# Two of the four weight sums of every pair, made by accumulating transfers of GpSimd instead of by VectorE

## The chip, the cores and the metric

The kernel runs on one core of a Trainium2 chip. The metric is the device time of one execution in microseconds (us). The time before is the median of three runs, 1945.45 us (1944.91 to 1946.29).

The core has five engines with instruction streams of their own: PE (the matrix engine), DVE (VectorE), ACT (ScalarE), POOL (GpSimd) and SP (SyncE, which here only issues transfers). Each takes its instructions in order and waits at semaphores for the others. Transfers are issued by an engine and carried out by 16 DMA engines.

## The reference

Two layers of a decoder trunk for 512 tokens and 1024 channels, all in fp32. Each layer projects the normed input once, runs three token mixers beside each other, merges them by gates, and ends in a feed-forward part of four times the width:

```
h = rms_norm(x, norm1[l]) * (1.0 + sc1) + sh1
proj = h @ w_in[l]
q, k, v, g, u, vs, p, gate_cols = split_columns(proj)
y_ret  = retention(q, k, v, g, positions)
y_sgu  = spatial_gating(u, vs, ws_gmlp[l], bs_gmlp[l], vnorm_gmlp[l])
y_pool = multiscale_pool(p, w_pool[l], b_pool[l], pool_scale[l])
branch_proj = einsum('bsnc,ncd->bsnd', stack([y_ret, y_sgu, y_pool]), w_branch[l])
gates  = sigmoid(gate_cols.reshape(B, S, 3, D_MODEL))
x = x + gt1 * (sum(gates * branch_proj) @ w_out[l])
h2 = rms_norm(x, norm2[l]) * (1.0 + sc2) + sh2
x = x + gt2 * (square(relu(h2 @ w_ff1[l])) @ w_ff2[l])
```

The modulation vectors sc1, sh1, gt1 and so on are products of a conditioning vector with w_ada.

## The kernel before

**Weights as units.** All weights stream from HBM in units of 128 partitions x 1024 values (512 KB), in the order in which they are used, on SP's queue (`load_raw`, L229, its transfer in L237). Each fp32 product is made of three faster ones (`mm3`, L401, its matmul in L407), so every unit and every activation is split in two: ACT copies the high half (`whi`), then DVE subtracts it from the raw values to get the low half (`wlo`; `split_unit`, L243). A plain unit gives one 128-column block of the output; it takes 24 matmuls of 512 columns.

**Pairs.** Two neighbouring units of the gates and of most of the first feed-forward matrix are computed together with seven half-size products in place of eight, by a scheme of sums (44 pairs, 22 per layer). With r1 and r2 as the two raw units and a, b as their left and right halves, DVE makes four sums of 128 x 512 (L218 in the profile, since all go through the helper `ttn`): s[a] = r2[a] + r2[b]; s[b] = s[a] - r1[a]; then in place r1[a] = r1[a] - r2[a] and r1[b] = r1[b] - s[b]. Four things are split per pair, in four groups: r1 as loaded (W1a, W1b), s (S1, S2), the changed r1 (S3, S4), and r2[b] (W2b). The activations have sums of the same kind, T1 to T4 (`Halved.add`, L139; the tiles `tpart`). `pair` (L419) runs the products in the order W1a, S1, S2, W1b, S3, S4, W2b, twelve matmuls of 256 columns each, into PSUM tiles a and d (`ps`) and b and c (`us`); between them ACT copies a into b (`us<-ps`) and b into c, and DVE adds d to b and to c (`gate<-us,d` or `pair<-us,d`).

**What sets the order.** The steps of a layer are listed (`step`), and `run` (L323) emits them one by one, with a look-ahead of two units or groups: `load_until` issues loads and splits ahead of the products, and the modulation units (`mod`, one DVE product over a whole unit in L257, then two or three small operations of `finish_mod`, on POOL for two columns of layer 0 at the start, else on DVE) are mixed in. From this the framework's scheduler fixes one instruction order per engine. Gates of the second branch come as single pairs between plain units. Those of the third begin with one pair and then three that stand together, and the pairs of the feed-forward matrix stand in runs of three, four and three. In such runs the last groups of one pair are split while the sums of the next are made.

**Pools.** Raw units rotate through 4 buffers (`wraw`), split units through 4, s through 1 (`sums`), small 512-column tiles through 8 (`tmp`). A load into a buffer waits until its last reader is done.

Of the kernel before, what the change touches and what calls it, by code (L numbers as in the profile page):

```python
# [11 lines left out]
F32 = mybir.dt.float32  # L12
F32R = mybir.dt.float32r
I32 = mybir.dt.int32
AF = mybir.ActivationFunctionType
ALU = mybir.AluOpType

P = 128
D = 1024
# [72 lines left out]
class Split:  # L92


    def __init__(self, pool, name):
        self.pool, self.name = pool, name
        self.t = {}
# [34 lines left out]
class Halved:  # L132
# [6 lines left out]
    def add(self, p, f=None):  # L139

        b = self.b
        if f is None:
            f = []
            for k2 in (p, p + KB // 4):
                f.append(b.b4("f32"))
                hi, lo = (self.act.two(w, k2).bitcast(F32) for w in ("hi", "lo"))
                b.ttn(f[-1], hi, lo, ALU.add)
        upper, lower = f
        r11, r12, r21, r22 = upper[:, :, :HT], upper[:, :, HT:], lower[:, :, :HT], lower[:, :, HT:]
        raws = [b.b4("tsum").rearrange("p a (k s) -> p a k s", k=2) for _ in range(2)]  # L150
        t1, t2, t3, t4 = (raws[i // 2][:, i % 2] for i in range(4))
        b.ttn(t1, r12, r11, ALU.subtract)
        b.ttn(t2, r22, t1, ALU.subtract)
        b.ttn(t3, r22, r12, ALU.subtract)
        b.ttn(t4, r21, t2, ALU.subtract)
        for names, raw in zip((("T1", "T2"), ("T3", "T4")), raws):
            hi, lo = (b.big.tile([P, 2, 2, HT], F32R, tag="b4", name=b.name("tpart")) for _ in range(2))
            b.act(hi, raw, AF.Copy)
            b.ttn(lo, raw, hi.bitcast(F32), ALU.subtract)
            for i, n in enumerate(names):  # L160
                self.sums[n, p] = [t[:, i] for t in (hi, lo)]
# [9 lines left out]
class Builder:  # L171
    def __init__(self, tc, ctx, ins, out, wstream, order):
        self.tc, self.nc = tc, tc.nc
        self.ins, self.out = ins, out
        self.wstream = wstream
        self.order = order
        self.steps = []
        self.const = ctx.enter_context(tc.tile_pool(name="const", bufs=1))
        self.big = ctx.enter_context(tc.tile_pool(name="big", bufs=BIG_BUFS))
        self.wraw = ctx.enter_context(tc.tile_pool(name="wraw", bufs=4))  # L180
        self.whl = ctx.enter_context(tc.tile_pool(name="whl", bufs=UNIT_BUFS))
        self.sums = ctx.enter_context(tc.tile_pool(name="sums", bufs=1))
        self.dram = ctx.enter_context(tc.tile_pool(name="dram", bufs=1, space=bass.MemoryType.DRAM))
        self.tmp = ctx.enter_context(tc.tile_pool(name="tmp", bufs=8))
        self.psum = ctx.enter_context(tc.tile_pool(name="psum", bufs=6, space=bass.MemoryType.PSUM))
        self.seeded = ctx.enter_context(tc.tile_pool(name="seeded", bufs=2, space=bass.MemoryType.PSUM))
        self.n_t = 0
# [82 lines left out]

    def load_pair(self, keys):

        r1, r2 = (self.load_raw(k) for k in keys)
        a, b = slice(0, S), slice(S, D)
        got = []

        def make(group):
            if group == 0:
                return self.split_unit(r1)
            if group == 1:  # L280
                s = self.sums.tile([P, D], F32, tag="sum", name=self.name("sum"))
                got.append(s)
                self.ttn(s[:, a], r2[:, a], r2[:, b], ALU.add)
                self.ttn(s[:, b], s[:, a], r1[:, a], ALU.subtract)
                return self.split_unit(s)
            if group == 2:
                self.ttn(r1[:, a], r1[:, a], r2[:, a], ALU.subtract)
                self.ttn(r1[:, b], r1[:, b], got[0][:, b], ALU.subtract)
                return self.split_unit(r1)
            return self.split_unit(r2[:, b])  # L290

        return make

# [125 lines left out]
    def pair(self, form, mov, out, f, hooks={}):  # L419

        a, b, c, d = (x()[:, :HT] for x in (self.bank, self.ubank, self.ubank, self.bank))
        h0, h1 = HALVES
        d_sb = self.tt("d")[:, h0]

        def product(ps, w, m, start):  # L430
            if w in hooks:
                hooks[w]()
            hi, lo = form(w)
            for j in range(KB // 2):
                o = slice(j * P, (j + 1) * P)
                self.mm3(ps, hi[:, o], lo[:, o], *mov.parts(m, j), start and j == 0, j == KB // 2 - 1, loose=True)

        product(a, "W1a", "R11", True)
        self.act(b, a, AF.Copy)
        product(d, "S1", "T1", True)  # L440
        self.act(d_sb, d, AF.Copy)
        product(b, "S2", "T2", False)
        self.act(c, b, AF.Copy)
        product(a, "W1b", "R21", False)
        f(out[:, 0, h0], a)
        product(b, "S3", "T3", False)
        self.ttn(out[:, 1, h1], b, d_sb, ALU.add)
        product(c, "S4", "R22", False)
        self.ttn(out[:, 0, h1], c, d_sb, ALU.add)
        product(b, "W2b", "T4", False)  # L450
        f(out[:, 1, h0], b)
# [747 lines left out]
    def final(self, i, units, between=None):  # L1199
        nc = self.nc  # L1200
        tok = HALVES[i]

        def pair(k2):
            def f():
                t = self.b4("fo")[:, :, tok]
                for j in range(2):
                    kb = 2 * k2 + j
                    self.stt(t[:, j, :], self.x[kb][:, tok], self.vecs[:, V_FN + kb:V_FN + kb + 1], ALU.mult,
                             self.rstd[:, tok], ALU.mult)
                o = self.out[k2 * 2 * P:(k2 + 1) * 2 * P, tok].rearrange("(a p) s -> p a s", p=P)  # L1210
                nc.sync.dma_start(out=o, in_=t)
            return f

        pair(0)()
        if between is not None:
            between()
        return [pair(k2) for k2 in range(1, KB // 2)]
# [91 lines left out]
```

## Time and profile before

| what | value |
|---|---|
| median of 3 runs | 1945.45 us |
| the profiled execution | 1946.67 us, span 1945.0 us |
| DMA packets | 77803, 263.18 MB |
| HBM read, written | 246.81 MB, 14.68 MB |
| q1 (all that SP issues) | 261.52 MB, 41.5% of 16 engines |

The page of the profile gives busy times of each engine, 40 slices of the span, the queues, the chain that ended last and the costliest groups. In a row of a group, the numbers behind the bar are busy us and mean ns of one, and behind a second bar the idle time just before them with what ended most of it. In a row of the timeline, the numbers are start and duration in us, and a bracket at the end holds the idle time before it and its releaser. Rows of DMA issues end in the size of one and the median us from issue to landing. Names are tiles of the program without their numbers.

### The profile page before, as it was taken

What the parts mean: (1) busy time and instruction counts of PE and PEld (TensorE: products, weight loads), DVE (VectorE), ACT (ScalarE), POOL (GpSimd) and SP (SyncE); (2) the same over time, 40 slices, a digit from 0 to 9 for tenths busy, and PEclk for the clock granted to TensorE, in tenths of its full rate; (3) what the DMA queues carried; (4) which work ended last, traced back from release to release, by engine and by line L of the source; (5) the groups of instructions that cost most, each with busy time, mean ns of one, the idle gap of its engine ahead of it and who ended that gap; (6) DMA issues with size and microseconds to landing.
All of it is one profiled execution on the core that took longest, in us unless ns stands there. A gap on an engine that the chain in (4) does not pass through costs nothing.

```text
span 1945.0 us, 25939 instructions
## 1 busy us (share of the span) xinstructions
PE 1923.6 (99%) x10424; PEld 1656.4 (85%) x10424; DVE 1291.9 (66%) x1913; ACT 814.7 (42%) x1156; POOL 19.9 (1%) x46
## 2 busy tenths in 40 slices
PE   8999999999999999999999999999999999999998
PEld 5889977888888888898888898778889898899896
DVE  7888657776864776676555775676587557455555
ACT  4444323443443544363434333334335337254452
POOL 2000000000000000000000000000000000000000
PEclk9999999999999999999999999999999999999999
DMA  9454633373242353453425456313523424232331
GB/s 354 152 173 152 214 112 108 108 251 118 98 152 87 106 176 108 152 164 119 130 87 180 145 182 202 114 55 108 185 84 111 141 79 149 87 120 72 124 98 54
DMA packets 77803, 263.18 MB, mean 135 GB/s; under 512 B 8305, under 2 KB 14577, under 8 KB 77682
## 3 DMA queue, kind: packets, MB, share of 16 engines
q1 hardware_dynamic: 77682, 261.52, 41.5%
q8 instruction: 81, 1.33, 0.3%
q14 instruction: 40, 0.33, 0.1%
HBM read 246.81 MB, written 14.68 MB: 134 GB/s over the span
## 4 chain that ended last, share of the span: by engine, by line
PE 91%; DVE 4%; ACT 2%; DMA 2%; issue 1%; POOL 0%; DVEq 0%; ACTq 0%
PE ps L407 73%; PE us L407 14%; PE ps L800 2%; DMA raw<-in_weights 2%; DVE wlo L218 1%; PE ps L778 1%; ACT whi L221 1%; DVE raw L257 1%; PE ps L920 0%; PE ps L1023 0%; PE ps L813 0%; ACT pair L221 0%; ACT sq L221 0%; DVE ysg L215 0%; DVE tpart L218 0%
## 5 line engine op out<-in xcount | busy, mean ns | idle before, releaser
L221 ACT ACTIVATE whi<-raw 128x1024 fp32r<-128x1024 f32 (+1 forms) x384 | 385.6, 1008 | 699.1 <-PE ps L407 415.8
L218 DVE TENSOR_TENSOR wlo<-raw,whi 128x1024 fp32r<-128x1024 f32 (+1 forms) x384 | 443.7, 1160 | 193.5 <-ACT whi L221 186.5
L407 PE MATMUL ps<-h_hi,whi 128*128 128x512 f32 (+1 forms) x704 | 258.6, 367 | 0.0
L407 PE MATMUL ps<-h_hi,wlo 128*128 128x512 f32 (+1 forms) x704 | 254.0, 361 | 0.0
L407 PE MATMUL ps<-h_lo,whi 128*128 128x512 f32 (+1 forms) x704 | 253.6, 360 | 0.0
L407 PE MATMUL ps<-hid_hi,whi 128*128 128x512 f32 (+1 forms) x544 | 204.6, 378 | 0.3 <-ACT whi L221 0.2
L407 PE MATMUL ps<-hid_lo,whi 128*128 128x512 f32 (+1 forms) x544 | 204.3, 377 | 0.0
L407 PE MATMUL ps<-hid_hi,wlo 128*128 128x512 f32 (+1 forms) x544 | 203.9, 377 | 0.0
L407 PE MATMUL us<-tpart,whi 128*128 128x256 f32 x1056 | 196.4, 284 | 3.1 <-ACT us L221 1.6
L407 PEld LDWEIGHTS us<-tpart,whi 128*128 128x128 f32 x1056 | 167.6, 191 | 9.3 <-ACT us L221 2.2
L257 DVE CUSTOM_DVE_ANT_0 raw<-raw,cact 128x1024 f32<-128x1024 f32 x96 | 117.3, 1223 | 82.7 <-DMA raw<-in_weights 82.5
L407 PEld LDWEIGHTS ps<-h_hi,whi 128*128 128x128 f32 x704 | 132.9, 189 | 21.4 <-issue 1.4
L407 PEld LDWEIGHTS ps<-h_lo,whi 128*128 128x128 f32 x704 | 132.9, 189 | 21.4 <-issue 1.4
L407 PEld LDWEIGHTS ps<-h_hi,wlo 128*128 128x128 f32 x704 | 132.8, 189 | 20.6
L407 PE MATMUL us<-tpart,wlo 128*128 128x256 f32 x528 | 149.4, 283 | 0.0
L215 DVE SCALAR_TENSOR_TENSOR x<-ps,mod,x 128x512 f32<-128x512 f32 (+1 forms) x88 | 61.2, 700 | 132.4 <-PE ps L407 132.0
L407 PEld LDWEIGHTS ps<-hid_hi,whi 128*128 128x128 f32 x544 | 102.4, 188 | 19.1 <-ACT whi L221 0.7
L407 PEld LDWEIGHTS ps<-hid_hi,wlo 128*128 128x128 f32 x544 | 102.4, 188 | 18.5
L407 PEld LDWEIGHTS ps<-hid_lo,whi 128*128 128x128 f32 x544 | 102.4, 188 | 18.3
L407 PE MATMUL ps<-hh_lo,whi 128*128 128x256 f32 (+1 forms) x344 | 111.8, 325 | 0.0
L407 PE MATMUL ps<-hh_hi,wlo 128*128 128x256 f32 (+1 forms) x344 | 111.7, 325 | 0.0
L407 PE MATMUL ps<-hh_hi,whi 128*128 128x256 f32 (+1 forms) x344 | 111.1, 328 | 0.5
(224 smaller groups left out, 3661.0 us busy)
## 6 DMA issues: line engine op xcount, KB each, us to landing
raw<-in_weights SPq DMA_DIRECT2D x436, 512.0 KB, 3.6
parked<-merged SPq DMA_DIRECT2D x16, 512.0 KB, 2.9
merged<-parked SPq DMA_DIRECT2D x16, 512.0 KB, 5.1
v<-v SPq DMA_DIRECT2D x8, 512.0 KB, 6.2
vh<-v SPq DMA_DIRECT2D x8, 512.0 KB, 5.7
x<-in_xT SPq DMA_DIRECT2D x8, 256.0 KB, 3.7
dec<-in_decay SPq DMA_DIRECT2D x4, 512.0 KB, 4.9
out_dram<-fo SPq DMA_DIRECT2D x8, 256.0 KB, 2.2
```

Of the source, the lines that this page charges most:

```text
L215: self.nc.vector.scalar_tensor_tensor(out, in0, sc, in1, op0, op1)
L218: self.nc.vector.tensor_tensor(out, a, b, op)
L221: self.nc.scalar.activation(out, in_, f, **k)
L257: self.nc.vector.tensor_tensor_reduce(out=raw, in0=raw, in1=self.cact, scale=0.5, scalar=0.0, op0=ALU.mult, op1=ALU.add, accum_out=acc)
L407: mm(ps, lhsT=l, rhs=r, start=start and i == 0, stop=stop and i == 2, skip_group_check=loose)
L778: nc.tensor.matmul(ps[:, :w], lhsT=k[:, j * P:(j + 1) * P], rhs=q[:, j * P:], start=True, stop=True)
L800: nc.tensor.matmul(ps[:, j * P:], lhsT=st["v", hd][:, j, e * P:(e + 1) * P], rhs=sc[j], start=j == 0, stop=j == NCH - 1)
```

## The change

Per pair, x (the former s) and v (the former changed r1, now a tile of its own) come from the pool `sums`, which has 2 buffers, so exactly one pair's x and v; `tmp` goes from 8 to 7. SP loads r1 in full, then x[a] = r2[a] and v[a] = r1[a] as base loads of 256 KB each. Then POOL issues two accumulating transfers of 256 KB: x[a] += r2[b] and v[a] += r2[a], straight from HBM; each waits for its base load. Last, SP loads r2[b] alone. DVE makes x[b] = x[a] + r1[a] and v[b] = r1[b] + x[b]. A few signs flip with it: in the sums of the activations, in two copies of ACT (scale -1.0), and in one addition that becomes a subtraction.

```
-            self.sums = ctx.enter_context(tc.tile_pool(name="sums", bufs=1))
+            self.sums = ctx.enter_context(tc.tile_pool(name="sums", bufs=2))
-            self.tmp = ctx.enter_context(tc.tile_pool(name="tmp", bufs=8))
+            self.tmp = ctx.enter_context(tc.tile_pool(name="tmp", bufs=7))
...
     def load_pair(self, keys):
-        r1, r2 = (self.load_raw(k) for k in keys)
         a, b = slice(0, S), slice(S, D)
-        got = []
+        i1 = len(self.order)
+        i2 = i1 + 1
+        r1 = self.load_raw(keys[0])
+        self.order.append(keys[1])
+        w1, w2 = self.wstream[i1], self.wstream[i2]
+        nc = self.nc
+        x, v = (self.sums.tile([P, D], F32, tag="sum", name=self.name("sum")) for _ in range(2))
+        nc.sync.dma_start(out=x[:, a], in_=w2[:, a])
+        nc.sync.dma_start(out=v[:, a], in_=w1[:, a])
+        nc.gpsimd.dma_start(out=x[:, a], in_=w2[:, b], accum_op=ALU.add)
+        nc.gpsimd.dma_start(out=v[:, a], in_=w2[:, a], accum_op=ALU.add)
+        r2 = self.wraw.tile([P, D], F32, tag="raw", name=self.name("raw"))[:, b]
+        nc.sync.dma_start(out=r2, in_=w2[:, b])
 
         def make(group):
             if group == 0:
                 return self.split_unit(r1)
             if group == 1:
-                s = self.sums.tile([P, D], F32, tag="sum", name=self.name("sum"))
-                got.append(s)
-                self.ttn(s[:, a], r2[:, a], r2[:, b], ALU.add)
-                self.ttn(s[:, b], s[:, a], r1[:, a], ALU.subtract)
-                return self.split_unit(s)
+                self.ttn(x[:, b], x[:, a], r1[:, a], ALU.add)
+                return self.split_unit(x)
             if group == 2:
-                self.ttn(r1[:, a], r1[:, a], r2[:, a], ALU.subtract)
-                self.ttn(r1[:, b], r1[:, b], got[0][:, b], ALU.subtract)
-                return self.split_unit(r1)
-            return self.split_unit(r2[:, b])
+                self.ttn(v[:, b], r1[:, b], x[:, b], ALU.add)
+                return self.split_unit(v)
+            return self.split_unit(r2)
...
     def pair(self, form, mov, out, f, hooks={}):
-        self.act(b, a, AF.Copy)
+        self.act(b, a, AF.Copy, scale=-1.0)
-        self.act(c, b, AF.Copy)
+        self.act(c, b, AF.Copy, scale=-1.0)
-        self.ttn(out[:, 1, h1], b, d_sb, ALU.add)
+        self.ttn(out[:, 1, h1], b, d_sb, ALU.subtract)
```

Over the program DVE has 88 operations fewer, SP 88 transfers more (512 to 600), and POOL 88 transfers where it had none. PE's products stay as they are. In the order of DVE's instructions the change shows as follows, at the three places that the prediction calls A, B and C. Numbers tell tiles of one name apart; they differ between the two programs.

**Place A**, on DVE, where the last steps of the spatial gating's u run and the first pair of the second gates is being split (layer 0; `ysg` is a block of the mixed u, `ISA` the product of a modulation unit). Before:

```order
L218 TENSOR_TENSOR wlo_208_1245<-sum_206_1241,whi_207_1244 128x1024
L218 TENSOR_TENSOR ysg_197_1189<-ysg_197_1189,gu_173_1049 128x512
L218 TENSOR_TENSOR ysgu0_lo1_1194<-ysg_197_1189,ysgu0_hi1_1192 128x512
L215 SCALAR_TENSOR_TENSOR ysg_205_1236<-ps_204_1231,vecs_85,mix_107_623 128x512
L218 TENSOR_TENSOR wlo_226_1341<-raw_198_1196,whi_225_1340 128x1024
L218 TENSOR_TENSOR ysg_205_1236<-ysg_205_1236,gu_179_1086 128x512
L218 TENSOR_TENSOR ysgu0_lo1_1194<-ysg_205_1236,ysgu0_hi1_1192 128x512
L257 ISA raw_237_1422,acc0_98<-raw_237_1422,cact_102 128x1024
```

And now:

```order
L257 ISA raw_238_1425,acc0_98<-raw_238_1425,cact_102 128x1024
L257 ISA acc0_98 128x1
L215 SCALAR_TENSOR_TENSOR ysg_197_1189<-ps_196_1184,vecs_85,mix_107_623 128x512
L218 TENSOR_TENSOR wlo_209_1249<-sum_199_1198,whi_208_1248 128x1024
...
L215 SCALAR_TENSOR_TENSOR ysg_207_1242<-ps_206_1237,vecs_85,mix_107_623 128x512
L218 TENSOR_TENSOR wlo_227_1344<-sum_200_1199,whi_226_1343 128x1024
L218 TENSOR_TENSOR sum_240_1445<-sum_240_1445,raw_239_1443 128x512
L218 TENSOR_TENSOR ysg_207_1242<-ysg_207_1242,gu_179_1086 128x512
L218 TENSOR_TENSOR sum_241_1446<-raw_239_1443,sum_240_1445 128x512
L218 TENSOR_TENSOR ysgu0_lo1_1194<-ysg_207_1242,ysgu0_hi1_1192 128x512
L218 TENSOR_TENSOR wlo_229_1361<-raw_201_1204,whi_228_1360 128x512
```

The add of the next pair (sum_240, which waits for the accumulating transfer into a tile that is free once wlo_209 is made) now stands ahead of the ysg product, and the modulation product ahead of wlo_209. Before, the next pair's first sum came some fifteen operations later.

**Place B**, on DVE, between the first two of three neighbouring pairs of the third gates (layer 0; `ypool` is the pooling branch, `mrg` the merged sum). Before:

```order
L218 TENSOR_TENSOR wlo_724_4382<-sum_722_4378,whi_723_4381 128x1024
...
L218 TENSOR_TENSOR sum_740_4503<-raw_737_4484 128x512
L218 TENSOR_TENSOR sum_740_4503<-sum_740_4503,raw_736_4482 128x512
L215 SCALAR_TENSOR_TENSOR gate_688_4161<-gate_688_4161,ps_721_4347 128x512
L218 TENSOR_TENSOR wlo_733_4436<-raw_716_4337,whi_732_4435 128x1024
L215 SCALAR_TENSOR_TENSOR gate_688_4161<-gate_688_4161,ps_725_4385 128x512
L218 TENSOR_TENSOR merged_707_4287<-merged_707_4287,gate_688_4161 128x512
L218 TENSOR_TENSOR wlo_735_4453<-raw_717_4339,whi_734_4452 128x512
L218 TENSOR_TENSOR wlo_739_4487<-raw_736_4482,whi_738_4486 128x1024
L218 TENSOR_TENSOR merged_707_4287<-merged_707_4287,gate_688_4161 128x512
L218 TENSOR_TENSOR wlo_742_4507<-sum_740_4503,whi_741_4506 128x1024
```

And now:

```order
L218 TENSOR_TENSOR wlo_734_4413<-sum_726_4366,whi_733_4412 128x1024
...
L218 TENSOR_TENSOR sum_747_4514<-sum_747_4514,raw_746_4512 128x512
L218 TENSOR_TENSOR merged_716_4314<-merged_716_4314,gate_697_4189 128x512
L218 TENSOR_TENSOR wlo_743_4466<-sum_727_4367,whi_742_4465 128x1024
L215 SCALAR_TENSOR_TENSOR gate_697_4189<-gate_697_4189,ps_735_4416 128x512
L218 TENSOR_TENSOR wlo_745_4483<-raw_728_4372,whi_744_4482 128x512
L218 TENSOR_TENSOR mrg0_lo0_4409<-merged_716_4314,mrg0_hi0_4407 128x512
L218 TENSOR_TENSOR sum_748_4515<-raw_746_4512,sum_747_4514 128x512
L218 TENSOR_TENSOR merged_716_4314<-merged_716_4314,gate_697_4189 128x512
L218 TENSOR_TENSOR wlo_751_4523<-raw_746_4512,whi_750_4522 128x1024
L218 TENSOR_TENSOR wlo_753_4541<-sum_747_4514,whi_752_4540 128x1024
```

The add (sum_747) stands ahead of the remaining halves of the current pair (wlo_743, wlo_745) and of both first halves of the next (wlo_751, wlo_753).

**Place C**, on DVE, between the second and third of three neighbouring pairs of the feed-forward part (layer 0; `hid` is the hidden activation). Before:

```order
L218 TENSOR_TENSOR wlo_1117_7145<-sum_1115_7141,whi_1116_7144 128x1024
L218 TENSOR_TENSOR pair_1103_7058<-us_1106_7061,d_1108_7063 128x256
L218 TENSOR_TENSOR wlo_1119_7164<-raw_1111_7120,whi_1118_7163 128x1024
L218 TENSOR_TENSOR sum_1132_7269<-raw_1129_7250 128x512
L218 TENSOR_TENSOR wlo_1127_7219<-raw_1112_7122,whi_1126_7218 128x512
L218 TENSOR_TENSOR sum_1132_7269<-sum_1132_7269,raw_1128_7248 128x512
L218 TENSOR_TENSOR wlo_1131_7253<-raw_1128_7248,whi_1130_7252 128x1024
L218 TENSOR_TENSOR hid0_2_lo2_7183<-pair_1103_7058,hid0_2_hi2_7182 128x1024
L257 ISA raw_1148_7382,acc1_99<-raw_1148_7382,cact_102 128x1024
```

And now:

```order
L218 TENSOR_TENSOR wlo_1135_7200<-sum_1129_7173,whi_1134_7199 128x1024
L218 TENSOR_TENSOR pair_1120_7109<-us_1123_7112,d_1125_7114 128x256
L218 TENSOR_TENSOR wlo_1137_7218<-sum_1130_7174,whi_1136_7217 128x1024
L218 TENSOR_TENSOR wlo_1145_7273<-raw_1131_7179,whi_1144_7272 128x512
L218 TENSOR_TENSOR sum_1147_7304<-sum_1147_7304,raw_1146_7302 128x512
L218 TENSOR_TENSOR hid0_2_lo2_7237<-pair_1120_7109,hid0_2_hi2_7236 128x1024
L218 TENSOR_TENSOR sum_1148_7305<-raw_1146_7302,sum_1147_7304 128x512
L257 ISA raw_1167_7439,acc1_99<-raw_1167_7439,cact_102 128x1024
L257 ISA acc1_99 128x1
L218 TENSOR_TENSOR wlo_1151_7313<-raw_1146_7302,whi_1150_7312 128x1024
```

The low half of the next pair's first unit (wlo_1151, formerly wlo_1131) now stands behind the add, hid's low half, the sum for v and a modulation product.

At the start, SP's two base loads of the first pair stand ahead of weights of the first projection, and POOL's two accumulating transfers between the small operations that finish the second and the third of eight modulation columns.

More of the change, by code (lines that the diff above doesn't have):

```diff
@@ L151, in add @@
         t1, t2, t3, t4 = (raws[i // 2][:, i % 2] for i in range(4))
-        b.ttn(t1, r12, r11, ALU.subtract)
-        b.ttn(t2, r22, t1, ALU.subtract)
-        b.ttn(t3, r22, r12, ALU.subtract)
+        b.ttn(t1, r11, r12, ALU.subtract)
+        b.ttn(t2, r22, t1, ALU.add)
+        b.ttn(t3, r12, r22, ALU.subtract)
         b.ttn(t4, r21, t2, ALU.subtract)
```

## The prediction

> **What bounds the kernel now.** I read the page first, then the waits of the matrix engine, then the chain of work that ended last.
>
> ```profile
> span 1945.0 us, 25939 instructions
> PE 1923.6 (99%) x10424; PEld 1656.4 (85%) x10424; DVE 1291.9 (66%) x1913; ACT 814.7 (42%) x1156; POOL 19.9 (1%) x46
> PE 91%; DVE 4%; ACT 2%; DMA 2%; issue 1%; POOL 0%; DVEq 0%; ACTq 0%
> PE us L407 <- ACT us L221: 1.6, 3, 0.7
> PE us L407 <- DVE pair L218: 1.5, 2, 1.2
> PE ps L407 <- ACT whi L221: 0.7, 2, 0.6
> PE ps L407 <- DVE wlo L218: 0.7, 3, 0.3
> ```
>
> PE is busy 99% of the span. DVE has a third of its time free, and POOL is idle. The last four lines are waits of PE in L407, where all weight products run: total us, times, longest. They add to 4.5 us. The change leaves PE's instructions and their number alone, so it can gain little, and any new wait of PE is a full loss: this is the frame for all that follows.
>
> **What DVE loses.** The groups of DVE by form show the four sums of a pair and the low half of its sum tile:
>
> ```profile
> L218 DVE TENSOR_TENSOR raw<-raw,raw 128x512 f32<-128x512 f32 x44 | 30.3, 688 | 0.5
> L218 DVE TENSOR_TENSOR sum<-raw 128x512 f32<-128x512 f32 x44 | 30.2, 687 | 23.4 <-DMA raw<-in_weights 23.2
> L218 DVE TENSOR_TENSOR sum<-sum,raw 128x512 f32<-128x512 f32 x44 | 30.2, 685 | 0.4
> L218 DVE TENSOR_TENSOR raw<-raw,sum 128x512 f32<-128x512 f32 x44 | 30.1, 684 | 0.0
> ```
>
> 44 pairs with four sums each. Two of the four go: 88 x 0.686 = 60.4 us of DVE, 4.7% of its busy time. Since PE waits for DVE or ACT only 4.5 us in these products, this is worth 4.5 us at most. Of these, 1.1 us fall at the places treated below and are counted there; of the 3.4 left I take **-2.5**. (Starts on DVE lie closer together than the durations: 1.13 for a 128x1024 and 0.60 for a 128x512 operation, which I use in chains below.)
>
> **What the transfers cost.** Per pair SP now issues r1 (512 KB) and three of 256 KB, and POOL two of 256 KB that add into a tile: 768 KB more are read per pair, 44 x 768 KB = 34.6 MB in all.
>
> ```profile
> GB/s 354 152 173 152 214 112 108 108 251 118 98 152 87 106 176 108 152 164 119 130 87 180 145 182 202 114 55 108 185 84 111 141 79 149 87 120 72 124 98 54
> q1 hardware_dynamic: 77682, 261.52, 41.5%
> raw<-in_weights SPq DMA_DIRECT2D x436, 512.0 KB, 3.6
> v<-v SPq DMA_DIRECT2D x8, 512.0 KB, 6.2
> x<-in_xT SPq DMA_DIRECT2D x8, 256.0 KB, 3.7
> out_dram<-fo SPq DMA_DIRECT2D x8, 256.0 KB, 2.2
> ```
>
> [...] Only the first slice runs at the highest rate shown, 354 GB/s. There the first pair's 1 MB of base loads and accumulating transfers now goes ahead of weights that PE waits for: 3.0 us if all of it shows, nothing if the queue has slack. I take **+1**. The finishing of the modulation columns on POOL comes every 5.27 us there (its scaling takes 1.83 us), and two issues of POOL now stand in between:
>
> ```profile
> 26.73 1.83 POOL L305 TENSOR_SCALAR mod<-acc,vecs 128x1 f32<-128x1 f32 x1 [3.03 <-DVE acc L257]
> ```
>
> POOL was idle for 3.03 us before it, which covers both issues; without that cover they cost some 2 us, once.
>
> What decides is the **latency of the accumulating transfer**, from POOL's issue to landing; I call it X. The trace of before has none. The nearest rows are 2.2 us (256 KB stored) and 6.2 us (512 KB, the slowest such form shown often), and these are the bounds of X. [...] I take **X = 4.3**, nearest to the weights' row. The base load of 256 KB, which must land first, I take at 2.7, between 2.2 and 3.7. So from the moment that the tile of the previous pair is free, the new add on DVE can start **7.0 us** later; between 4.4 (2.2 + 2.2) and 9.9 (3.7 + 6.2) it may be anything.
>
> [...]
>
> **Where 7.0 us is too long.** The order shows that in every pair DVE's add stands ahead of the low half of the pair's first unit, and often of other work. DVE takes its instructions in order, so all behind the add waits too. I walk three places.
>
> Place C, two neighbouring pairs of the feed-forward part in layer 0:
>
> ```profile
> 837.76 1.22 DVE L218 TENSOR_TENSOR wlo<-sum,whi 128x1024 fp32r<-128x1024 f32 x1
> 843.78 1.22 DVE L218 TENSOR_TENSOR wlo<-raw,whi 128x1024 fp32r<-128x1024 f32 x1 [1.54 <-ACT whi L221]
> 846.30 1.23 DVE L257 CUSTOM_DVE_ANT_0 raw<-raw,cact 128x1024 f32<-128x1024 f32 x1
> 847.17 0.28 PE L407 MATMUL ps<-hh_hi,wlo 128*128 128x256 f32 x1
> 849.13 0.50 PE L407 MATMUL us<-tpart,whi 128*128 128x256 f32 x2 [0.37 <-DVE pair L218]
> 852.50 0.51 PE L407 MATMUL us<-tpart,whi 128*128 128x256 f32 x2 [0.47 <-ACT us L221]
> ```
>
> The first row ends at 838.98: the old x tile is free. The new x can be added to at 838.98 + 7.0 = 845.98. Behind the add (0.60) stand now hid's low half (1.13), the sum for v (0.60), a modulation product (1.15) and only then the first unit's low half (1.14): 850.6. In the trace of before that half was made at 843.78, and PE first uses it at 847.17. It would come 3.4 us late; PE lost 0.37 + 0.47 = 0.84 there already: **+2.6**. In layer 1 no modulation product stands between: 1.2 less, **+1.4**. Where hid's half is not between either, the half comes at 848.3, about 1 us late, which the 0.84 lost before nearly pays; these seven or so handovers I count as even.
>
> Place B, three consecutive pairs of the third gates:
>
> ```profile
> 519.08 1.22 DVE L218 TENSOR_TENSOR wlo<-sum,whi 128x1024 fp32r<-128x1024 f32 x1
> 531.80 1.22 DVE L218 TENSOR_TENSOR wlo<-sum,whi 128x1024 fp32r<-128x1024 f32 x1
> 533.08 0.39 PE L407 MATMUL ps<-tpart,wlo 128*128 128x256 f32 x1 [0.28 <-DVE wlo L218]
> ```
>
> The tile is free at 520.2, the add can start at 527.2. From there to the end of the next low half of x DVE has, in the new order, two 128x1024 halves of the raw unit and v and that of x (3 x 1.14) and seven operations of 128x512 (0.60 to 0.67): 527.2 + 3.4 + 4.3 = 534.9. Before, it ended at 533.02 with PE already waiting. So 1.9 us late; for the second handover, closer behind, I estimate 1.0: 2.9 per layer, **+5.8**.
>
> Place A, the steps of the spatial gating's u just before the second gates, layer 0:
>
> ```profile
> 148.72 1.21 DVE L218 TENSOR_TENSOR wlo<-sum,whi 128x1024 fp32r<-128x1024 f32 x1
> 153.89 0.69 DVE L218 TENSOR_TENSOR ysg<-ysg,gu 128x512 f32<-128x512 f32 x1
> 163.21 0.37 ACT L221 ACTIVATE us<-ps 128x256 f32<-128x256 f32 x1
> 163.79 0.40 PE L407 MATMUL us<-tpart,whi 128*128 128x256 f32 x2
> ```
>
> A modulation product now stands ahead of the freeing row: free at 149.93 + 1.15 = 151.1, the add at 158.1, while DVE arrives about 155. Behind the add stand a ysg product that was made at 153.89, the sum for v, two low halves, two drains of PSUM and two more ysg products (5.6 us with the add): 163.7. ACT makes a ysg high half (0.57) and then the copy us<-ps (0.37) for which PE waits: 164.7 against 163.79, **+1** (0.9). In layer 1 without the product: nothing.
>
> **Held transfers.** SP's queue is in order: the two base loads wait for DVE to have split the old x and v, and r2 and the next units wait behind them.
>
> ```profile
> 839.22 1.22 DVE L218 TENSOR_TENSOR wlo<-raw,whi 128x1024 fp32r<-128x1024 f32 x1
> ```
>
> This row is the low half of v at place C: v is free at 840.4, 1.5 us after x, so that r2 lands by 845; its product is the pair's last, some 7 us after the first use at 847.17. I cost this at nothing; without that cover it costs what X would. The flipped signs change no instruction's shape, and tmp's eighth buffer is named by no wait of PE: nothing, up to +1.
>
> **Sum:** -2.5 + 1 + 2.6 + 1.4 + 5.8 + 1 = +9.3 us. The profiled execution took 1946.67 us, 1.2 above the median of 1945.45, and the sum from it gives 1956.0; against the median, 1954.8. I forecast **1955 us**.
>
> **Rivals.** The order is fixed, so X decides between them.
> - The accumulating transfer is quick: at X = 2.2 to 3.3 the add at place C comes at 843.9 to 845.0, about when DVE idles anyway (the 1.54 us before 843.78). No handover is late, the relief stands: 1945.45 - 4.5 = **1941**, faster. For it: the store's 2.2 us, and queues that are 41.5% full. Against it: most rows of 256 and 512 KB have 3.6 and more. Chance 0.22. [...]
> - It nets out: X near 3.6. Each of the seven late handovers (one at A, four like B, two like C) shrinks by up to 0.7 us, so up to 4.9 of 10.8 us go: 9.3 - 4.9 = +4.4, or less where DVE catches up; **1942 to 1949**. Chance 0.18.
> - It is slow: X = 6.2, as v<-v, because the add is slow or POOL's issue is. Then 1.9 us more at each of 20 handovers inside runs of pairs and at the two of place A: 1955 + 22 x 1.9 = **1997**. For it: POOL's 1.83 us for a trifle. Against: isolated pairs have slack. Chance 0.20.
> - The change doesn't free DVE, because DVE idles in the new wait for as long as it saved: true in my forecast too, and it shows in DVE's rows, not in another time.
>
> **How the numbers follow.** The forecast (1949.4 to 1975) has 0.40, the rivals 0.22, 0.18 and 0.20. A measurement of this kernel can tell about 0.2%, 3.9 us, from no change. Faster: 0.22; within: 0.18; slower: 0.40 + 0.20 = 0.60. The range goes from the quick rival, 1940, to most of the slow one, 1990; beyond lie some 0.05 below and 0.12 above.
>
> **What would show it.** DVE busy falls by about 60 us. DVE rows of the add (sum<-sum,raw) gain idle time before them, put down to the accumulating DMA: 2 to 4 us at places like A, B, C. The median from issue to landing of the 88 POOL transfers is X, and settles which rival it is: under 3.3 quick, over 5.5 slow. PE's waits for wlo, whi and us grow from 4.5 us to some 14, near 163, 533 and 850 us. HBM reads rise by about 34.6 MB. The forecast is wrong if X is 4 to 4.5 and PE yet waits no more than now (then my walk of DVE's order is wrong), or if the time moves without these waits (then it is startup, or held loads on SP).

## The result, and the profile after

The changed kernel takes 2000.87 us (median of 4, 1997.05 to 2003.74) against 1945.87: ratio 1.0282, interval 1.0270 to 1.0295. It is 55 us slower, beyond the range given (1940 to 1990). The page of the changed kernel, for comparison with the lines shown before:

```profile
span 1999.3 us, 26318 instructions
PE 1938.7 (97%) x10424; PEld 1667.5 (83%) x10424; DVE 1240.9 (62%) x1825; ACT 814.4 (41%) x1156; POOL 96.8 (5%) x134
HBM read 281.41 MB, written 14.68 MB: 148 GB/s over the span
raw<-in_weights SPq DMA_DIRECT2D x392, 512.0 KB, 4.0
sum<-in_weights SPq DMA_DIRECT2D x88, 256.0 KB, 3.0
sum<-in_weights POOLq DMA_DIRECT2D x88, 256.0 KB, 5.3
```

DVE is busy 51 us less, HBM reads are up by 34.6 MB, and the accumulating transfer takes 5.3 us from issue to landing at the median, between the signs that the prediction had set for its own X (4 to 4.5) and for the slow rival (over 5.5). The span has grown by 54.3 us, in two parts. The first shows in the waits of PE (total us, times, longest):

```profile
PE ps L414 <- DVE wlo L218: 18.9, 11, 3.1
PE ps L414 <- ACT whi L221: 13.3, 10, 2.9
PE us L414 <- ACT us L221: 7.8, 4, 2.3
PE us L414 <- DVE pair L218: 1.3, 1, 1.3
```

These are the four lines of before, which had 4.5 us; now they have 41.3. All idle gaps of PE of at least 0.2 us, added up from the timeline, are 50.7 us against 11.2: **+39.5 us**. The second part is PE's busy time itself, 1938.7 against 1923.6 for the same 10424 matmuls: **+15.1 us**. 39.5 + 15.1 = 54.6, which is the growth of the span to 0.3 us.

The groups of DVE by form show where DVE waits:

```profile
L218 DVE TENSOR_TENSOR sum<-sum,raw 128x512 f32<-128x512 f32 x44 | 30.4, 691 | 117.1 <-DMA sum<-in_weights 106.9 <-DMA raw<-in_weights 10.1
```

The add of x now has 117 us of idle time ahead of it, 107 of them until an accumulating transfer landed; the first sum of a pair had 23.4 us before, for loads. One of these waits can be followed through four engines. Between two single pairs of the second gates, in layer 0, the timeline has on SP, POOL, DVE and PE:

```profile
206.74 0.33 SPq L281 DMA_DIRECT2D sum<-in_weights  x1
210.78 0.86 POOL L283 DMA_DIRECT2D sum<-in_weights  x1 [23.05 <-DVE mod L317]
205.50 1.21 DVE L218 TENSOR_TENSOR wlo<-sum,whi 128x1024 fp32r<-128x1024 f32 x1
217.20 0.69 DVE L218 TENSOR_TENSOR sum<-sum,raw 128x512 f32<-128x512 f32 x1 [5.59 <-DMA sum<-in_weights]
218.54 2.35 DVE L218 TENSOR_TENSOR wlo<-raw,whi 128x1024 fp32r<-128x1024 f32 x2
219.81 0.50 PE L414 MATMUL ps<-ysgu_hi,wlo 128*128 128x512 f32 x1 [3.12 <-DVE wlo L218]
```

DVE frees the old x at 206.71 (205.50 + 1.21), and SP issues the base load 0.03 us later. POOL issues the accumulating transfer 4.0 us after that, and 6.4 us later DVE can add. The two low halves behind the add belong to the next plain units, which have nothing to do with the pair. PE, which needs one of them, stands still for 3.12 us.

What follows explains the second part. The windows of the same stretch, for PE alone (length and busy us, matmuls, granted clock, DMA share, GB/s; a packet counts where it starts, so a share can pass 1):

```profile
216.00:218.00 2.00, 0.69 (x6) 1.00 1.10 257
218.00:220.00 2.00, 0.19 (x1) 1.00 0.11 17
220.00:222.00 2.00, 2.00 (x7) 0.67 0.32 113
222.00:224.00 2.00, 2.00 (x7) 0.50 0.96 354
224.00:226.00 2.00, 2.00 (x13) 0.97 0.46 94
```

After the stall the granted clock is half for 3.4 us, in which PE gets half its work done: 1.7 us more are lost. The granted clock of the whole run shows nine such stretches, two of them back to back, outside the kernel's last microseconds, and one in the kernel before, near 28 us: 8 x 1.7 = 13.7 of the 15.1 us.

### The profile page after: what moved, and what is told of

The parts are those of the page before. It is cut to its first block, busy times and chain, and to the rows that moved or that the text cites. A ratio compares the mean times of both kernels' runs of the same rounds, so it can differ in the third digit from the quotient of the medians.

```text
span 1999.3 us, 26318 instructions
## 1 busy us (share of the span) xinstructions
PE 1938.7 (97%) x10424; PEld 1667.5 (83%) x10424; DVE 1240.9 (62%) x1825; ACT 814.4 (41%) x1156; POOL 96.8 (5%) x134
## 3 DMA queue, kind: packets, MB, share of 16 engines
q0 software_dynamic: 12672, 23.07, 7.2%
## 5 line engine op out<-in xcount | busy, mean ns | idle before, releaser
L221 ACT ACTIVATE whi<-raw 128x1024 fp32r<-128x1024 f32 (+1 forms) x340 | 339.7, 1002 | 649.2 <-PE ps L414 433.7
L218 DVE TENSOR_TENSOR wlo<-raw,whi 128x1024 fp32r<-128x1024 f32 (+1 forms) x340 | 390.3, 1152 | 184.2 <-ACT whi L221 173.4
L414 PE MATMUL ps<-h_hi,whi 128*128 128x512 f32 (+1 forms) x704 | 259.5, 369 | 2.0 <-ACT whi L221 2.0
L414 PE MATMUL ps<-h_hi,wlo 128*128 128x512 f32 (+1 forms) x704 | 254.9, 362 | 0.0
L414 PE MATMUL ps<-h_lo,whi 128*128 128x512 f32 (+1 forms) x704 | 254.4, 361 | 0.0
L414 PE MATMUL us<-tpart,whi 128*128 128x256 f32 x1056 | 198.9, 286 | 9.0 <-ACT us L221 7.8
L414 PE MATMUL ps<-hid_hi,whi 128*128 128x512 f32 (+1 forms) x544 | 204.9, 378 | 1.5 <-ACT whi L221 1.4
L414 PE MATMUL ps<-hid_lo,whi 128*128 128x512 f32 (+1 forms) x544 | 205.0, 377 | 0.0
L414 PE MATMUL ps<-hid_hi,wlo 128*128 128x512 f32 (+1 forms) x544 | 204.4, 377 | 0.0
L414 PEld LDWEIGHTS us<-tpart,whi 128*128 128x128 f32 x1056 | 169.2, 193 | 15.1 <-ACT us L221 8.6
L221 ACT ACTIVATE whi<-sum 128x1024 fp32r<-128x1024 f32 x88 | 93.1, 1059 | 171.0 <-PE ps L414 74.3
L414 PEld LDWEIGHTS ps<-h_hi,whi 128*128 128x128 f32 x704 | 133.9, 190 | 23.6 <-ACT whi L221 2.4
L414 PEld LDWEIGHTS ps<-h_lo,whi 128*128 128x128 f32 x704 | 133.9, 190 | 21.3 <-issue 1.4
L414 PEld LDWEIGHTS ps<-h_hi,wlo 128*128 128x128 f32 x704 | 133.7, 190 | 20.4
L414 PE MATMUL us<-tpart,wlo 128*128 128x256 f32 x528 | 150.2, 284 | 0.0
L414 PEld LDWEIGHTS ps<-hid_hi,whi 128*128 128x128 f32 x544 | 102.4, 188 | 21.0 <-ACT whi L221 2.6
L414 PE MATMUL ps<-hh_hi,wlo 128*128 128x256 f32 (+1 forms) x344 | 113.2, 329 | 6.7 <-DVE wlo L218 6.7
L414 PEld LDWEIGHTS ps<-hid_lo,whi 128*128 128x128 f32 x544 | 102.4, 188 | 18.4
L414 PEld LDWEIGHTS ps<-hid_hi,wlo 128*128 128x128 f32 x544 | 102.2, 188 | 18.4
L218 DVE TENSOR_TENSOR wlo<-sum,whi 128x1024 fp32r<-128x1024 f32 x88 | 107.1, 1220 | 13.1 <-ACT whi L221 12.3
```

Source lines behind the costliest of these rows:

```text
L218: self.nc.vector.tensor_tensor(out, a, b, op)
L221: self.nc.scalar.activation(out, in_, f, **k)
L414: mm(ps, lhsT=l, rhs=r, start=start and i == 0, stop=stop and i == 2, skip_group_check=loose)
```

## The experiments

Theory T: the transfer into a sum's tile starts when the old tile is free, lands some 8 us later, and DVE's order puts other low halves behind the add that waits for it. Rival R: the additional bytes slow the weight loads. All ratios are against the kernel before, run on the same chip. PE waits given below are of its L413 or L414.

**Third buffer.** One more tile for x and v, so that a pair's x has its place before the current x is split:

```
-BIG_BUFS = 31
+BIG_BUFS = 30
-            self.sums = ctx.enter_context(tc.tile_pool(name="sums", bufs=2))
+            self.sums = ctx.enter_context(tc.tile_pool(name="sums", bufs=3))
```

> The changed kernel with a third buffer for x and v (the pool of the activations gives one of its 31 up), nothing else. Theory T (the accumulating transfer can only start when the old tile is free, and lands some 8.3 us later, 3.0 of base load and 5.3 of accumulation; DVE's order puts other low halves behind the add): with a third buffer the next x has its tile without waiting for the current x, so most of the 55 us go, 1948 to 1962 us, and the DVE idle time before the add falls from 117 us to under 60. Rival R (the 768 KB more per pair and the read-back slow all weight loads): the traffic is the same, so it stays at 1990 to 2000 us.

1956.41 us, ratio 1.0048 (1.0033 to 1.0063). The group of the add, and the transfer, in this run:

```profile
sum<-in_weights POOLq DMA_DIRECT2D x88, 256.0 KB, 5.7
```

```profile
L218 DVE TENSOR_TENSOR sum<-sum,raw 128x512 f32<-128x512 f32 x44 | 30.4, 691 | 78.8 <-DMA raw<-in_weights 48.9 <-issue 18.2 <-DMA sum<-in_weights 11.6
```

With the same bytes and a transfer that is no quicker (5.7 us), 44 of the 55 us are gone. The idle time ahead of the add is 78.8 us, more than the 60 expected, but only 11.6 of it end with the accumulating transfer, instead of 106.9. R's own sign doesn't move: the 512 KB loads of weights take 4.0 us here as in the change (3.6 before). R keeps at most the last 10 us. (The profiled execution took 1951.89 us, the quickest of the four.)

The third buffer also lets the scheduler move 25 of the 44 adds forward in DVE's order, ahead of one to four more low halves, so the two orders are not the same. At the place followed above, however, DVE's instructions from the old x's low half to the two low halves behind the add are the same in both. There the add starts after this wait:

```profile
211.95 0.69 DVE L218 TENSOR_TENSOR sum<-sum,raw 128x512 f32<-128x512 f32 x1 [2.72 <-DMA raw<-in_weights]
```

It waits for r1 and no longer for the transfer, and PE's stall behind it is 0.34 us in place of 3.12.

**DVE adds.** The change's base loads, without its accumulating transfers:

```
-        nc.gpsimd.dma_start(out=x[:, a], in_=w2[:, b], accum_op=ALU.add)
-        nc.gpsimd.dma_start(out=v[:, a], in_=w2[:, a], accum_op=ALU.add)
...
             if group == 1:
+                self.ttn(v[:, a], v[:, a], x[:, a], ALU.add)
+                self.ttn(x[:, a], x[:, a], r2, ALU.add)
                 self.ttn(x[:, b], x[:, a], r1[:, a], ALU.add)
```

> The changed kernel without its accumulating transfers: base loads of x[a] and v[a] by SP as they are, and DVE adds to them, four sums per pair again; pools, signs and buffers of the change. T: the add waits for 3.0 us of base load only, 1945 to 1955 us, and the PE waits for wlo and whi shrink from 32 us to under 8. R: 256 KB of the 768 KB more per pair remain, so about a third of the loss, 1964 us.

1965.33 us, ratio 1.0108 (1.0089 to 1.0127): the time that R gave, and not T's; PE's waits for low and high halves are 16.4 us, where T had under 8. But the first sum here reads v's base load, whose tile comes free after x's, and it stands ahead of all; T could have this too:

```profile
PE ps L414 <- DVE wlo L218: 15.0, 11, 3.2
L218 DVE TENSOR_TENSOR sum<-sum,sum 128x512 f32<-128x512 f32 x44 | 30.4, 691 | 52.7 <-DMA sum<-in_weights 52.4
```

The next run separates the two.

**DVE adds, third buffer.** The same with 3 buffers for x and v and 30 for activations.

> The run with DVE's additions on base loads, with the third buffer for x and v added. T (what costs is a load that can start only when the old tile is free): the 20 us that this layout lost without any accumulating transfer go, 1944 to 1952 us, and the 15.0 us of PE waits for wlo fall below 3. R (more bytes, more transfers on the queue): the bytes are the same, 1960 to 1966 us.

1951.75 us, ratio 1.0039 (1.0026 to 1.0052).

```profile
PE ps L414 <- DVE wlo L218: 6.0, 3, 3.3
L218 DVE TENSOR_TENSOR sum<-sum,sum 128x512 f32<-128x512 f32 x44 | 30.4, 691 | 39.5 <-DMA sum<-in_weights 36.1 <-issue 2.9 <-DVE wlo L218 0.5
```

With every byte of the run before, two thirds of its loss are gone, and PE's waits for wlo fall from 15.0 to 6.0 us, not below 3 as expected. So most of this loss isn't the traffic. A load behind a tile's release, even a plain one of 2.8 us, fits it; but DVE's order differs between these two runs as well (34 of the 44 first sums stand earlier here), and the runs don't part the two.

**Signs and tmp.** The kernel before with the signs flipped and seven tmp buffers; DVE makes its four sums where it did.

```
-            self.tmp = ctx.enter_context(tc.tile_pool(name="tmp", bufs=8))
+            self.tmp = ctx.enter_context(tc.tile_pool(name="tmp", bufs=7))
...
-        self.act(b, a, AF.Copy)
+        self.act(b, a, AF.Copy, scale=-1.0)
```

> The kernel before with only the flipped signs and seven tmp buffers. T and R: no difference, 1944 to 1948 us. If the tmp pool or the scaled copies carry part of the loss, it shows here as more than 4 us.

1946.05 us, ratio 1.0001 (0.9992 to 1.0011). They carry nothing beyond the 2 us of the interval.

**Plain transfers of GpSimd.** Both transfers lose their `accum_op=ALU.add` and so write over the base loads.

> The changed kernel with both GpSimd transfers made plain copies (the additions r2[a] + r2[b] and r1[a] + r2[a] are left out); order, queues and bytes read from HBM as in the change. If the accumulation makes X long (the destination is read back), X falls from 5.3 us to about 3.5 to 4.0 and the time to 1950 to 1972 us. If it is GpSimd's issue that makes X long, X stays near 5 and the time within 10 us of 2000.

1969.65 us, ratio 1.0119 (1.0104 to 1.0135).

```profile
sum<-in_weights POOLq DMA_DIRECT2D x88, 256.0 KB, 3.6
```

3.6 us against 5.3 for the accumulating form and 2.9 for SP's loads of the same size in this run. The accumulation makes the transfer 1.7 us longer, and these cost 31 us of time. At 3.6 us, the length at which the prediction let the change net out, 24 us are still lost. DVE's order is that of the change but for two operations.

**Only x, only v.** One of the two sums by an accumulating transfer each; r2 is loaded whole, and DVE makes the other sum, for only v as it made s before:

```
-        nc.gpsimd.dma_start(out=x[:, a], in_=w2[:, b], accum_op=ALU.add)
+        nc.sync.dma_start(out=r2, in_=w2)
...
+                self.ttn(x[:, a], r2[:, a], r2[:, b], ALU.add)
                 self.ttn(x[:, b], x[:, a], r1[:, a], ALU.add)
```

> Only x[a] is made by an accumulating transfer; r2 is loaded whole, DVE adds v[a] = r1[a] + r2[a]; two buffers. T: x is the sum that is needed first and waited for ahead of other low halves, so most of the loss stays, 1970 to 1995 us. R: per pair 512 KB more in place of 768 KB, two thirds of the loss, 1982 us.

> Only v[a] is made by an accumulating transfer; r2 is loaded whole and DVE makes x as it made s before; two buffers. T: v is split some 5 us of PE time after x, and its sum on DVE doesn't wait for the transfer, so hardly anything is lost, 1942 to 1952 us, with DVE idle before x's sum as before the change (23 us and not 117). R: per pair 512 KB more, as with only x, 1982 us: the two runs would be alike.

Only x: 2001.98 us, ratio 1.0290 (1.0274 to 1.0305). Only v: 1943.74 us, ratio 0.9993 (0.9983 to 1.0002). Waits of PE and DVE's group of only x:

```profile
PE ps L413 <- DVE wlo L218: 25.6, 13, 5.0
PE us L413 <- ACT us L221: 6.9, 2, 4.8
```

```profile
L218 DVE TENSOR_TENSOR sum<-sum,raw 128x512 f32<-128x512 f32 x44 | 30.4, 692 | 113.7 <-DMA sum<-in_weights 100.9 <-DMA raw<-in_weights 12.7
```

And DVE's group of the first sum in only v:

```profile
L218 DVE TENSOR_TENSOR sum<-raw 128x512 f32<-128x512 f32 x44 | 30.4, 690 | 48.4 <-DMA raw<-in_weights 47.8
```

Both read the same 269.88 MB with the same number of transfers, and one loses 57 us, more than expected and as much as the change, the other nothing. The accumulation of v, which no sum of DVE waits for (ACT and DVE split v later), is free; with that of x, for which an add waits in the middle of DVE's order, the whole loss is there. R, which made both alike, falls.

The two runs differ in more than that. In only v DVE idles 48.4 us before x's first sum, not the 23 expected, though for whole units and not for a sum's tile; against only x, 20 of the 44 first sums stand one or two low halves later there and 8 one earlier. In only x DVE's own sum for v waits 15.6 us for r2.

**GpSimd adds.** The change with x[b] and v[b] made by GpSimd, so that DVE has no add that waits:

```
-                self.ttn(x[:, b], x[:, a], r1[:, a], ALU.add)
+                nc.gpsimd.tensor_tensor(x[:, b], x[:, a], r1[:, a], ALU.add)
```

> The change with the sums for x[b] and v[b] made by GpSimd, so that DVE waits at no add; buffers and transfers as in the change. If the loss comes from what stands behind the add in DVE's order (low halves of other units), 20 us or more come back, 1965 to 1982 us, and PE waits for wlo at plain units (near 195, 220, 1183 and 1209 us) vanish. If it comes from x itself being late, GpSimd's slower add makes it later still: 2000 us or more.

1972.93 us, ratio 1.0136 (1.0121 to 1.0151).

```profile
PE ps L414 <- ACT whi L221: 14.5, 9, 3.5
PE us L414 <- ACT us L221: 4.0, 5, 1.1
PE ps L414 <- DVE wlo L218: 3.1, 7, 0.8
```

GpSimd's add takes 1.5 us in place of 0.69, so x is later than in the change (from the base load's issue to the end of the add 11.9 us at the median of all pairs, against 10.6), and yet 28 us come back: PE's waits for low halves fall from 18.9 to 3.1 us, and those near 195, 220, 1183 and 1209 us are gone, as expected. What stood behind the add was about half the loss, or more, since x is later. The waits for whi and us remain, where x's own lateness shows, or ACT's order.

**Four buffers, and the rest.** Four tiles for x and v need two of the activations' pool, so the kernel before was run with 29 there too; and only v was run with a third buffer.

```
-BIG_BUFS = 31
+BIG_BUFS = 29
-            self.sums = ctx.enter_context(tc.tile_pool(name="sums", bufs=2))
+            self.sums = ctx.enter_context(tc.tile_pool(name="sums", bufs=4))
```

> The changed kernel with four buffers for x and v (two pairs' worth); the pool of the activations has 29 for it. T: with the third buffer some 10 us were left; if those come from v's tile, which still waits for its predecessor, a fourth takes most of them, 1945 to 1950 us. R: if they come from the 34.6 MB more and from slower weight loads, it stays at 1952 to 1957 us.

> The kernel before with only the activations' pool cut to 29, the control to the run with four buffers. T and R: 1945 to 1949 us; what it is above 1945.5 is the pool's share there.

> Only v[a] by an accumulating transfer, with the third buffer (activations' pool 30). T: x's tile no longer waits for anything, but nothing was lost with two buffers either, so 1940 to 1946 us, no more than 5 us below the kernel before since PE waits only 11 us in all there. R: 1944 or more, as with two buffers.

Four buffers: 1951.92 us, ratio 1.0032 (1.0020 to 1.0044). Before with 29: 1948.63, 1.0011 (1.0002 to 1.0020). Only v with three: 1947.08, 1.0003 (0.9994 to 1.0012). So with four buffers some 5 us are left, just between the two ranges expected, of which the smaller pool accounts for about 2. The trace puts the last 3 us at the start. There SP issues the base loads of two pairs between 15.9 and 20 us, where before it issued weights; PE then waits 2.9 us for `h_lo` (1.3 in the kernel before with 29) behind a modulation product whose unit lands late, and has half the clock for 6.8 us in place of 3.4: 1.6 + 1.7 = 3.3 us. In one trace this is seen, not tested. Only v with three came out above the 1946 expected: the third buffer gains nothing where nothing was lost. No version beats the kernel before: only v, the best, is within its uncertainty.

## Why the prediction was wrong

**What held.** PE sets the time, DVE loses the work that was worked out (51 us of busy time; 60.4 by durations, 53 by the 0.60 from start to start), and nothing is gained by it: only v, which frees DVE of 44 operations at no price, is 1.5 us under the kernel before, inside the interval, where I had -2.5 for all 88. The wait that takes the place of the removed work, its cause (tile freed, base load, accumulation) and its place (the add ahead of low halves in DVE's order) were named, and third buffer, only x, only v and GpSimd's adds each bear them out. The places named show too: PE waits at 165, 540 to 557 and 860 to 869 us. The rival "slow" had 1997 us and 0.20.

**The step that failed: the walk along the handovers.** I took 7.0 us from the free tile to the add at every pair, gave losses to three places, and let the other handovers and the single pairs of the second gates come out even. The gaps of PE, by stage, in us:

| stage | before | after | more | forecast |
|---|---|---|---|---|
| place A, both layers | 0.66 | 5.65 | +5.0 | +1 |
| second gates, single pairs | 0 | 9.67 | +9.7 | 0 |
| first gates | 0.56 | 2.57 | +2.0 | 0 |
| third gates (B) | 0.56 | 10.39 | +9.8 | +5.8 |
| feed-forward pairs (C) | 2.47 | 14.54 | +12.1 | +4.0 |
| start, and the rest | 6.93 | 7.84 | +0.9 | +1 |
| PE's busy time | | | +15.1 | 0 |

The second gates were the blind spot. "Isolated pairs have slack" is true of the pair, whose products come much later. But the add that waits for it stands in DVE's order ahead of the low halves of the plain units in between, and these are needed at once: the stall at 219.81 above. I had written that all behind the add waits, and then looked only at what belongs to a pair.

**Was the way mis-sized?** In part. For the 30 pairs whose add waited for its transfer, the time from SP's issue of the base load to POOL's issue is 3.7 us at the median (I had 2.7), from there to the add 4.5 (3.9 to 8.0; I had 4.3), 8.5 in all against my 7.0. The 5.3 us of the page are over both transfers of a pair; the 4.3 of the forecast was my estimate of X, which no run with two transfers per pair shows (their medians are 5.0 to 5.8). With plain transfers the same way is 7.4 us, nearly mine, and 24 us are lost where my sum had 9: so much the walk missed at its own length. The other 31 us came with the longer transfer; at the slow rival's price of 22 handovers, 1.5 us more would be 33 us, an estimate. And one number was wrong for a way that varies. Over 10 us it took in 8 of 30 pairs in the change, in 7 of 30 with only x, in 2 of 28 with plain transfers. In 7 of the 30 pairs the way took 10.5 to 12.6 us, and the gaps of PE right behind these 7 hold 17.4 of the 42.8 us of the table's first five rows. The windows of a quick and of a long one, from SP's issue to the add:

```profile
916.80:924.22 7.42, 7.42 (x35) 6.13 (x34) 1.97 (x2) 1.06 (x1) 0.86 (x1) 1.00 0.44 83
206.74:217.20 10.46, 9.95 (x78) 9.51 (x76) 4.37 (x8) 4.64 (x8) 1.74 (x2) 1.00 0.81 255
```

The last two columns are the DMA share and GB/s. The quick one has the queue nearly to itself; the long one shares it with 512 KB loads, at a share of 0.81. I had given bandwidth no weight beyond the start, which fits the average (the queues' shares are 42.0 and 7.2%, 49.2 in all, against 41.5 before) and not these moments: the share is 0.38 to 0.78 over the ways of the other 23 pairs and 0.63 to 0.89 over these 7. This relation was seen in such windows, not tested by itself.

**A missing term: the clock.** Stalls cost more than their length here, as shown above: 13.7 us that no term of mine had. The trace of before had it, after two waits of 1.1 and 1.3 us near 28 us.

**The rivals.** Slow came out in time, by another way: not 1.9 us more at each of 22 places, but 27 stalls of 0.3 to 3.1 us, and nine half-clock spells behind them. Quick, with its X of 2.2 to 3.3 us, lies below both measured forms, 3.6 us plain and 5.3 accumulating.

## What to carry to other kernels

Before work is moved from an engine to a transfer, look at what stands behind the instruction that will wait for it on the in-order engine, also when it belongs to other work, and give the transfer a tile that is free early: one more buffer was worth 44 us here, and choosing the sum that is needed late (v, not x) was worth all of it. Price such a wait by the slow quarter of the transfers and not by the median: here 8 of 30 ways took over 10 us, at a median of 8.5. Where PE sets the time, look at the granted clock behind its stalls too: here 21 of 37 gaps of 1.7 to 3.3 us, and all 6 longer ones, were followed by half the clock, at 1.7 us a spell.

## What the hardware showed

**Half the clock after short stalls.** In the thirteen traces of this case (start and end left out) I set PE's gaps of 1 us or more beside the granted clock of the next microseconds. Of 31 gaps under 1.7 us two were followed by the half clock, both next to a longer gap; of 37 from 1.7 to 3.3 us, 21 were; of 6 longer ones, all. Each spell of 3.41 us at half the clock cost 1.7 us, twice that where a second stall followed, as near 868 us.

Stalls of one length differed by where they fell. In each trace the spells begin and end on a grid of 3.41 us, to within 0.01 us: in the change three begin at 166.08, 220.70 and 558.62 us, 16 and 99 such steps apart. Of the 7014 stretches of that grid that ran at the full clock, all 23 in which PE idled 1.88 us or more were followed by the half clock, 3 of 13 with 1.60 to 1.86 us, and none of the others. The stall of 2.88 us at 1208.82 in the change fell into two stretches, at most 1.67 us into one, and cost no clock.

**Accumulating transfers.** 256 KB took 5.0 to 5.8 us from issue to landing where two follow each other (medians of four runs, 5.3 in the change), 4.0 to 4.6 with one per pair (only x, and only v with two and three buffers), GpSimd's plain copies 3.6, and SP's base loads 2.8 to 3.7. Each issue kept GpSimd busy for 0.87 us. The queue of accumulating transfers has 12672 packets, that of the plain ones 7040, for the same 23.07 MB, and they took 7.2% of the 16 DMA engines' span against 3.4%. That the destination is read back, as rival R and the run with plain transfers supposed, no run shows by itself.
